# A hybrid decoder layer on one core: the side chains' loads and stores go through GpSimd's DMA queue instead of SyncE's

## The chip, the cores and the metric

The kernel runs on one core of one Trainium2 chip. The metric is the device time of one execution in microseconds (us), from runs of the whole program; smaller is better. A profile is one execution taken by the hardware profiler; its times are counted from the first instruction of the span.

## What is computed

One layer of a decoder, for 256 prompt tokens and 8 sample tokens (one new token of each of 8 sequences), all in float32:

```
h = rms_norm(x, norm_w);  z = h @ w_in                 # 4096 -> 14368 columns
A: sliding-window attention, 8 heads x 128             # qa, ka, va, ga
B: trailing means over 2/4/8/16 positions, 1024 wide   # u, gb
C: gated DeltaNet, 16 heads x 128                      # q, k, v (conv(4) + SiLU), g, a, b
   prompt: chunked form with a triangular solve
   sample: state = state * exp(g); delta = (v - k.state) * beta
           state = state + k (x) delta; o = q.state    # per head and sequence, 128 x 128
mix = concat[A * silu(ga), B * silu(gb), C_norm * silu(g)]
y = rms_norm(x + mix @ w_out, final_norm_w)            # 4096 -> 4096
```

Outputs are y, the prompt's keys, values, pooling and convolution inputs and its delta state, and for the sample tokens the caches with the new row put in: the attention caches (8 x 2048 x 1024 for keys and for values) are copied but for their oldest row, and the 16 x 8 delta states are read, updated and written.

## The kernel before

**The stream.** Everything is built around one stream of matmuls on TensorE. The 264 tokens are the moving operand. There are 113 output tiles of 128 columns for the input projection (in the order a/b, 16 of k, then q, v, g for each of 16 heads, then the attention's, then the pooling's) and 32 for the output projection, each with 32 contraction tiles, dealt out in chunks of 8. A float32 product is made of three matmuls (`emit_main`, L518): upper part of the weights by the upper part of x, upper by lower, lower by upper. The weights come as 1 MB loads of two chunks (`raw`, three slots; `emit_loads`, L456). ScalarE casts a chunk to its upper part `wh`, VectorE subtracts to get the lower part `wl` (`emit_split`, L488). `wh` and `wl` have HB = 4 buffers each, so the splits run up to three chunks ahead of the matmuls. A load into a slot is issued when the second chunk of the load before it in that slot has been split. Behind it comes, at a rate that depends on the phase, a piece of 0.5 MB of the caches' copy from HBM to HBM (`emit_copy`, L476).

**The side chains.** What the heads need beside the stream (convolutions, delta rule, attention, pooling) is written as Python generators, one for each head or part, that all work in one pool of SBUF, `arena`. Between the chunks of the stream `step` (L1395) lets each chain go on to its next `yield`, as far as a planner finds time for it. The planner (`Model`, L80) holds an estimated time for each engine and for the last write and use of every column. It lets a step in when VectorE and ScalarE would end it before the splits of the chunks ahead are due, less a margin of 2 us. All engines run their instructions in the order in which this planner issued them, and wait by semaphores.

**Sample half of the delta rule** (`sample`, L1046). Two workers take the 32 halves (16 heads, 4 sequences each) in turn. A half loads the state (`sdT`, 256 KB), k and q spread over all partitions from small arrays in HBM (`s_k`, `s_q`, 256 KB each), and for the first half of a head it first stores q to HBM (`s_q<-small`). It waits with `due` (L290) until the planner expects its last load. Then come four products with k on VectorE, scalings on ScalarE, four updates of the state, the store of the new state (`o_ds`, 256 KB), and four products with q. The same buffers then serve the worker's next half, so its `sdT` load waits for that store to land.

**Other side transfers.** `load_decay` loads a head's decay row, spread over the partitions (`s_gc`, 128 KB), twice for each head; `ev_conv` (L608) stores the convolution's inputs (`o_cv`) and loads the sample's (`scT`) after every eighth tile; `delta` stores the final state (`o_dp`); `attn_s` (L1184) loads cache rows (`kg`, `vg`) and stores the new ones; `pool_u` and `pool_g` load and store for the pooling.

**Queues before.** Except for a few constants at the start that are issued from GpSimd, and one from ScalarE, all DMAs are issued from SyncE, named `self.sy` and also `self.ld` (L201). It issues them in order. A DMA waits for its operands, and also for the DMA eight places before it on its queue, whose semaphore it takes over. GpSimd does small work otherwise: in `ev_conv` it clears and copies the convolution's border, which ScalarE's first ACTIVATE of the convolution reads, and keeps copies of the sample columns; it computes powers for the norms.

Of the kernel before, what the change touches and what calls it, by code (L numbers as in the profile page):

```python
# [12 lines left out]
NP = 256            # prompt tokens  # L13
NB = 8              # sample tokens (one per sequence)
NT = NP + NB
NK = 32             # contraction tiles of the model width
KC = 8              # contraction tiles per chunk
# [10 lines left out]
def tile_plan():  # L28
    """Order of the output tiles of the input projection: (kind, index)."""
    plan = [("ab", 0)] + [("k", h) for h in range(CH)]  # L30
    for h in range(CH):
        plan += [("q", h), ("v", h), ("g", h)]
    for h in range(AH):
        plan += [("qa", h), ("ka", h), ("va", h), ("ga", h)]
    for g in range(4):
        plan += [("u", 2 * g), ("u", 2 * g + 1), ("gb", 2 * g), ("gb", 2 * g + 1)]
    return plan
# [37 lines left out]
class Model:  # L75
    """Estimated times (us) of the engines' queues, and of every column's last write and last use."""
# [7 lines left out]
    def span(self, ap):  # L84
        """The quarters of the partitions and the columns of a tile (the kernel's inputs and outputs are not followed)."""
# [31 lines left out]
    def op(self, eng, dur, outs, ins):  # L117
        t = max(self.t[eng], self.ready(outs, ins))
        # engines take turns at a PSUM bank
# [12 lines left out]
    def dma(self, out, in_):  # L132
        n = 4
        for x in out.shape:
            n *= x
        t = max(self.t["sy"], self.ready([out], [in_])) + .46
        self.t["sy"] = t
        self.t["dma"] = max(self.t["dma"], t + .65) + max(n / 359e3, .02)
        t = self.t["dma"] + .9
        self.done(t, [out], [in_])  # L140
        return t


class Meter:
    """An engine, with an estimate of the time that its instructions take (us)."""
# [5 lines left out]
    def __getattr__(self, name):  # L151
        f = getattr(self.eng, name)

        def run(*a, **k):
            if name == "dma_start":
                if self.key == "sy":
                    self.b.loaded = self.b.model.dma(k["out"], k["in_"])
# [21 lines left out]
class Chain:  # L179
    """A generator, the estimated time at which its last step is through, and its products yet to be issued."""  # L180
# [10 lines left out]
class Builder:  # L191
    def __init__(self, nc, tc, d, pools):
# [8 lines left out]
        self.sy = self.ld = Meter(self, "sy", nc.sync, 0.0, 0.0, 0.0)  # L201
# [44 lines left out]
    def get_all(self, *sizes):  # L246
        """All of them or none, so that no two chains wait for each other's space."""
# [42 lines left out]
    def due(self, loaded):  # L290
        """Until a load can be expected to be there."""
# [7 lines left out]
    def lose(self, t):  # L299
        """Time for ScalarE's tables."""  # L300
# [4 lines left out]
    def mm(self, out, lhsT, rhs, start=True, stop=True):  # L305
        """A side product: it is issued inside a later chunk of the stream."""
# [14 lines left out]
    def flush(self, every=True):  # L321
        """The side products whose operands can be expected to be there."""
# [74 lines left out]
    def late_const(self):  # L397
# [4 lines left out]
        # halves: silu(z) = (tanh(z/2) + 1) * z/2  # L402
        self.ts(self.cw, self.cw, 0.5, ALU.mult)
        # buffers of the delta-rule phase
# [12 lines left out]
    def setup_stream(self):  # L417
        self.chunks = []      # (m, first k tile, number of k tiles, load index, offset in the load's tiles)
        self.loads = []       # (m, first k tile, number of k tiles, last chunk served, place, load that frees it)
# [36 lines left out]
    def emit_loads(self, limit=None):  # L456
        """The loads whose place is free."""
# [54 lines left out]
    def main_bank(self, m):  # L512
        """The PSUM bank of an output tile, and the tile that had it before."""
# [4 lines left out]
    def emit_main(self, n):  # L518
# [3 lines left out]
        for i in range(nk):  # L522
# [8 lines left out]
            if m == 0:  # L531
                # rows 0 to 63: W's upper part by x; rows 64 to 127: its lower part by x's upper part
# [22 lines left out]
    def square_x(self, q):  # L555
        """Squares of four of the k tiles, summed into self.ssum."""
# [51 lines left out]
    def ev_conv(self, kind, h, ps):  # L608
# [18 lines left out]
        if cj == 7:  # L627
            self.sy.dma_start(out=self.d["o_cv"][:, ci * 88:(ci + 1) * 88], in_=cstage)
# [31 lines left out]
    def ev_ab(self, ps):  # L660
# [13 lines left out]
        # a_log -> -exp(a_log)  # L674
# [23 lines left out]
        self.sy.dma_start(out=self.s_gc, in_=a[0:CH, 0:NP])  # L698
        self.sy.dma_start(out=self.s_eb[0], in_=a[0:CH, NP:NT])
        self.sy.dma_start(out=self.s_eb[1], in_=a[32:48, NP:NT])  # L700
# [21 lines left out]
    def decay(self, h, gcb, D):  # L722
        """D[j, t, i] = exp(gc_i - gc_j) for i >= j, else 0."""
# [58 lines left out]
    def invert(self):  # L782
        """T = (I + A)^-1 of the 128 diagonal 32 x 32 blocks, one block per partition."""
# [32 lines left out]
    def assemble(self, hb):  # L816
        """E = T^T of the 128 x 128 tiles, from its 32 x 32 diagonal blocks, in place of U."""
# [90 lines left out]
    def delta(self, h, R, kd, D, o, S, X, sq):  # L908
# [60 lines left out]
        self.sy.dma_start(out=self.d["o_dp"][h], in_=S.ap[:, w[1]])  # L969
# [4 lines left out]
        # 128 eps (sum q^2 + eps)  # L974
# [19 lines left out]
        # the last reader of k, U and E has been issued: their place takes the head's output  # L994
# [16 lines left out]
    def sample_tab(self):  # L1011
        """Columns by (head, sequence), then rows on all partitions: e^g, k2 e^g beta, k beta."""
# [33 lines left out]
    def sample(self, h, f, Sb, kb, qb, jk, sm):  # L1046
# [4 lines left out]
        if f == 0:  # L1051
            self.sy.dma_start(out=self.s_q[h].rearrange("f d b -> d f b"),
# [24 lines left out]
        self.sy.dma_start(out=self.d["o_ds"][h, :, f * 512:(f + 1) * 512], in_=Sb.ap)  # L1077
# [91 lines left out]
    def have(self, k, buf):  # L1169
        """Row tile k of the mixed heads; those of attention come in two parts."""  # L1170
# [13 lines left out]
    def attn_s(self, h, rep):  # L1184
# [27 lines left out]
        for name, i in (("o_wk", 1), ("o_wv", 2)):  # L1212
            self.sy.dma_start(out=self.d[name][:, 2047, h * P:(h + 1) * P],
# [78 lines left out]
    def pool_u(self, t):  # L1292
# [3 lines left out]
        self.sy.dma_start(out=self.d["o_u"][t], in_=u.ap)  # L1296
# [72 lines left out]
    def load_res(self, i):  # L1369
        self.ld.dma_start(out=self.xr[i % 2].ap.rearrange("p (k n) -> p k n", k=4),  # L1370
                          in_=self.d["xT"][:, 4 * i:4 * i + 4, :])

    def finish_early(self):
        """What the last norm needs of the tiles but one."""
# [20 lines left out]
    def step(self, free=False):  # L1395
        """Each side chain goes on by a step, as far as VectorE and ScalarE have time beside the stream."""
# [39 lines left out]
    def tile_done(self, m):  # L1436
# [24 lines left out]
        else:  # L1461
            self.start(self.ev_plain(kind, i, ps), True)
            if kind == "va":
                def out_kv(i=i):
                    yield from self.wait(("va", i))
                    self.sy.dma_start(out=self.d["o_ka"][i], in_=self.z["ka", i].ap)
                    self.sy.dma_start(out=self.d["o_va"][i], in_=self.z["va", i].ap)
# [16 lines left out]
    def build(self):  # L1484
# [8 lines left out]
        # TensorE's clock rises while it is busy  # L1493
# [113 lines left out]
# the first output tiles go side by side through the contraction, while x comes in  # L1607
# [4 lines left out]
# pieces of the caches' copy per load of weights: keys' tiles, delta rule, attention, pooling, output  # L1612
# [137 lines left out]
```

## Time and profile before

| | before |
|---|---|
| median of 3 runs | 1835.51 us (1834.74 to 1837.76) |
| profiled execution, span from first to last instruction | 1828.2 us |
| around that span, against the median | 7.3 us |
| busy: TensorE (PE) | 1801.3 us, 99% |
| busy: VectorE (DVE) | 1298.7 us, 71% |
| busy: ScalarE (ACT) | 850.3 us, 47% |
| busy: GpSimd (POOL) | 192.8 us, 11% |
| moved by DMA | 519.66 MB, mean 284 GB/s; SyncE's queue 80.5% of the 16 DMA engines' time |

A share of busy time is an average over stages with different limits. A matmul counts as busy for longer than the next one takes to start behind it, so TensorE's 99% says that it seldom stands still, not that it runs at its peak. Where it stands still is read from views of single stages, from the list of waits (who waited, for whom, for how long), and from the queue of the engine that issues DMAs (SPq for SyncE's). The time of an idle engine that nobody waits for costs nothing.

### The profile page before, as it was taken

What the parts mean: (1) busy time and instruction counts of PE and PEld (TensorE: products, weight loads), DVE (VectorE), ACT (ScalarE), POOL (GpSimd) and SP (SyncE); (2) the same over time, 40 slices, a digit from 0 to 9 for tenths busy, and PEclk for the clock granted to TensorE, in tenths of its full rate; (3) what the DMA queues carried; (4) which work ended last, traced back from release to release, by engine and by line L of the source; (5) the groups of instructions that cost most, each with busy time, mean ns of one, the idle gap of its engine ahead of it and who ended that gap; (6) DMA issues with size and microseconds to landing.
All of it is one profiled execution on the core that took longest, in us unless ns stands there. A gap on an engine that the chain in (4) does not pass through costs nothing.

```text
span 1828.2 us, 38217 instructions
## 1 busy us (share of the span) xinstructions
PE 1801.3 (99%) x15120; PEld 1790.3 (98%) x15120; DVE 1298.7 (71%) x3155; ACT 850.3 (47%) x1442; POOL 192.8 (11%) x504
## 2 busy tenths in 40 slices
PE   9999999999999999999999999999999999999996
PEld 9999999999999999999999999999999999999995
DVE  7987879668789788787877778676655654444444
ACT  7644444455455455455544443434333444444442
POOL 1132560421011101111000000000000000000000
PEclk9999999999999999999999999999999999999998
DMA  9788897656787888879888888889888798888873
GB/s 322 263 289 295 272 234 260 237 198 234 262 327 269 286 305 313 304 267 319 323 312 306 313 308 297 284 283 333 306 299 288 274 339 302 295 294 303 297 240 118
DMA packets 109380, 519.66 MB, mean 284 GB/s; under 512 B 25408, under 2 KB 35872, under 8 KB 70272
## 3 DMA queue, kind: packets, MB, share of 16 engines
q1 hardware_dynamic: 108624, 516.71, 80.5%
q8 instruction: 118, 1.93, 0.4%
q0 software_dynamic: 432, 0.50, 0.1%
q14 instruction: 62, 0.51, 0.1%
q10 hardware_dynamic: 144, 0.02, 0.0%
HBM read 499.67 MB, written 152.50 MB: 357 GB/s over the span
## 4 chain that ended last, share of the span: by engine, by line
PE 88%; DVE 5%; DMA 4%; issue 1%; ACT 1%; SPq 1%; DVEq 0%; ACTq 0%
PE mps L540 27%; PE mps L541 27%; PE mps L542 27%; PE sps L307 4%; DVE arena L174 3%; DMA raw<-win 3%; DVE wl L174 2%; PE sps L311 1%; PE sps L541 1%; PE sps L540 1%; PE sps L542 1%; SPq L158 1%; DVE y L174 1%; DMA o_ds<-arena 0%; ACT wh L174 0%
## 5 line engine op out<-in xcount | busy, mean ns | idle before, releaser
L540 PE MATMUL mps<-xh,wh 128*128 128x264 f32 x3456 | 995.3, 288 | 2.0 <-ACT wh L174 2.0
L542 PE MATMUL mps<-xh,wl 128*128 128x264 f32 x3456 | 979.9, 284 | 1.7 <-DVE wl L174 1.6
L174 DVE TENSOR_TENSOR wl<-raw,wh 128x1024 fp32r<-128x1024 f32 (+1 forms) x581 | 704.5, 1214 | 389.7 <-ACT wh L174 382.4
L541 PE MATMUL mps<-xl,wh 128*128 128x264 f32 x3456 | 980.2, 284 | 0.0
L174 ACT CAST wh<-raw 128x1024 fp32r<-128x1024 f32 (+2 forms) x586 | 604.8, 1036 | 611.2 <-PE mps L541 471.7
L540 PEld LDWEIGHTS mps<-xh,wh 128*128 128x128 f32 x3456 | 652.1, 189 | 3.7 <-ACT wh L174 2.5
L541 PEld LDWEIGHTS mps<-xl,wh 128*128 128x128 f32 x3456 | 651.7, 189 | 0.2
L542 PEld LDWEIGHTS mps<-xh,wl 128*128 128x128 f32 x3456 | 648.8, 188 | 2.5 <-DVE wl L174 2.5
L174 DVE SCALAR_TENSOR_TENSOR arena<-arena 128x128 f32<-128x128 f32 (+5 forms) x882 | 264.6, 356 | 10.9 <-DMA arena<-s_k 4.2
L174 ACT ACTIVATE arena<-arena 128x128 f32<-128x128 f32 (+7 forms) x319 | 119.3, 401 | 143.3 <-DVE arena L174 140.8
L542 PE MATMUL mps<-mix,wl 128*128 128x264 f32 x512 | 145.7, 284 | 0.0
L542 PE MATMUL mps<-mixc,wl 128*128 128x264 f32 x512 | 145.7, 284 | 0.0
L540 PE MATMUL mps<-mixc,wh 128*128 128x264 f32 x512 | 145.5, 284 | 0.0
L540 PE MATMUL mps<-mix,wh 128*128 128x264 f32 x512 | 145.5, 284 | 0.0
L541 PE MATMUL mps<-mixc,wh 128*128 128x264 f32 x512 | 144.9, 283 | 0.0
L541 PE MATMUL mps<-mix,wh 128*128 128x264 f32 x512 | 144.8, 283 | 0.0
L174 POOL COPY arena<-arena 128x8 f32<-128x8 f32 (+5 forms) x192 | 67.8, 376 | 450.7 <-DVE arena L174 392.8
L540 PEld LDWEIGHTS mps<-mix,wh 128*128 128x128 f32 x512 | 96.2, 188 | 0.0
L540 PEld LDWEIGHTS mps<-mixc,wh 128*128 128x128 f32 x512 | 96.2, 188 | 0.0
L542 PEld LDWEIGHTS mps<-mixc,wl 128*128 128x128 f32 x512 | 96.1, 188 | 0.0
L542 PEld LDWEIGHTS mps<-mix,wl 128*128 128x128 f32 x512 | 96.1, 188 | 0.0
L541 PEld LDWEIGHTS mps<-mixc,wh 128*128 128x128 f32 x512 | 96.1, 188 | 0.0
(115 smaller groups left out, 1340.9 us busy)
## 6 DMA issues: line engine op xcount, KB each, us to landing
raw<-win SPq DMA_DIRECT2D x214, 1024.0 KB, 7.0
o_wk<-ck SPq DMA_DIRECT2D x128, 511.8 KB, 7.4
o_wv<-cv SPq DMA_DIRECT2D x128, 511.8 KB, 6.8
raw<-wout SPq DMA_DIRECT2D x58, 1024.0 KB, 5.3
arena<-kg SPq DMA_DIRECT2D x32, 320.0 KB, 6.7
arena<-vg SPq DMA_DIRECT2D x32, 320.0 KB, 7.1
arena<-sdT SPq DMA_DIRECT2D x32, 256.0 KB, 4.5
arena<-s_k SPq DMA_DIRECT2D x32, 256.0 KB, 4.5
```

The source lines that it names most:

```text
L158: return f(*a, **k)
L174: return f(*a, **k)
L307: self.put(lambda: self.t.matmul(out, lhsT=lhsT, rhs=rhs, start=start, stop=stop), out, [lhsT, rhs], 2)
L311: self.put(lambda: self.t.transpose(out, in_, self.ident[:k, :k]), out, [in_], 1)
L540: self.t.matmul(ps, lhsT=h[:, w], rhs=xh, start=(k == 0), stop=False)
L541: self.t.matmul(ps, lhsT=h[:, w], rhs=xl, start=False, stop=False)
L542: self.t.matmul(ps, lhsT=l[:, w], rhs=xh, start=False, stop=(k == NK - 1))
```

## The change

All transfers that belong to side chains move from SyncE's queue to GpSimd's: `self.ld` now means GpSimd, and stores of side chains that were written as `self.sy` become `self.ld`. SyncE keeps x, the weights, the caches' copies, the residual (`load_res`), the store of all k (`s_k<-small`), two copies of small states and the final output. The planner gets a formula for DMAs of GpSimd's queue: they occupy GpSimd for 0.6 us and land 2.0 us plus twice their bytes at 359 GB/s later. Comments are taken out.

```diff
@@ Model
-    def dma(self, out, in_):
+    def dma(self, out, in_, queue="sy"):
         n = 4
         for x in out.shape:
             n *= x
+        if queue == "g":
+
+            t = self.t["g"] = max(self.t["g"], self.ready([out], [in_])) + .6
+            self.t["dma"] += n / 359e3
+            t += 2.0 + 2 * n / 359e3
+            self.done(t, [out], [in_])
+            return t
         t = max(self.t["sy"], self.ready([out], [in_])) + .46
@@ Meter
-                if self.key == "sy":
-                    self.b.loaded = self.b.model.dma(k["out"], k["in_"])
+                if self.key in ("sy", "g"):
+                    self.b.loaded = self.b.model.dma(k["out"], k["in_"], self.key)
@@ Builder
-        self.sy = self.ld = Meter(self, "sy", nc.sync, 0.0, 0.0, 0.0)
+
+        self.sy = Meter(self, "sy", nc.sync, 0.0, 0.0, 0.0)
+        self.ld = self.g
@@ sample
-            self.sy.dma_start(out=self.s_q[h].rearrange("f d b -> d f b"),
+            self.ld.dma_start(out=self.s_q[h].rearrange("f d b -> d f b"),
...
-        self.sy.dma_start(out=self.d["o_ds"][h, :, f * 512:(f + 1) * 512], in_=Sb.ap)
+        self.ld.dma_start(out=self.d["o_ds"][h, :, f * 512:(f + 1) * 512], in_=Sb.ap)
@@ load_res
-        self.ld.dma_start(out=self.xr[i % 2].ap.rearrange("p (k n) -> p k n", k=4),
+        self.sy.dma_start(out=self.xr[i % 2].ap.rearrange("p (k n) -> p k n", k=4),
```

The same edit from `self.sy` to `self.ld` stands at the stores `o_cv`, `s_gc`, `s_eb`, `o_dp`, `o_wk` and `o_wv` (the new row), `o_u`, `o_ka` and `o_va`. The loads `sdT`, `s_k`, `s_q`, `s_gc`, `scT`, `s_eb`, `kg`, `vg`, `abias`, `spT` and `pw` were written with `self.ld` before and go along.

How the queues change in the sample half of the delta rule. SyncE before, some 490 to 510 us into the span; `win` are the weights, `ck` the cache that is copied, and the names in brackets are the semaphores waited for (DMAHW: an earlier DMA of SyncE, DVE: VectorE):

```order
L158 DMA raw_80<-win 128x2048 [waits DMAHW0_49,DVE_49]
L158 DMA o_wk<-ck 16x8188 [waits DMAHW1_49]
L158 DMA o_ds<-arena 128x512 [waits DMAHW2_49]
L158 DMA arena<-sdT 128x512 [waits DMAHW3_49,DMAHW2_49,DVE_49]
L158 DMA arena<-s_k 128x512 [waits DMAHW4_49]
L158 DMA s_q<-small 128x2x4 [waits DMAHW5_49]
L158 DMA arena<-s_q 128x512 [waits DMAHW6_49,DMAHW5_49]
L158 DMA raw_81<-win 128x2048 [waits DMAHW7_49,DVE_49]
L158 DMA o_wk<-ck 16x8188 [waits DMAHW0_49]
L158 DMA o_ds<-arena 128x512 [waits DMAHW1_49,DVE_49]
L158 DMA raw_79<-win 128x2048 [waits DVE_49]
```

SyncE in the changed kernel, in the same part of the program:

```order
L165 DMA raw_80<-win 128x2048 [waits DMAHW7_49,DMAHW5_49,DVE_49]
L165 DMA o_wk<-ck 16x8188
L165 DMA raw_81<-win 128x2048 [waits DMAHW1_49,DVE_49]
L165 DMA o_wk<-ck 16x8188 [waits DMAHW0_49]
L165 DMA raw_79<-win 128x2048 [waits DMAHW3_49,DVE_49]
L165 DMA raw_80<-win 128x2048 [waits DMAHW5_49,DMAHW2_49,DVE_49]
```

Between two weight loads stood a store, three loads and a store of q; now there is at most a copy.

GpSimd before, in the same part; `MEMSET arena 128x3` and the `COPY` of 128x8x3 behind it make the convolution's border:

```order
L174 COPY small<-arena 128x8 [waits DVE_49]
L174 MEMSET arena 128x3
L174 COPY arena<-arena 128x8x3 [waits PE_49]
L174 COPY arena<-arena 128x3 [waits DVE_49]
L174 COPY arena<-arena 128x8 [waits DVE_49]
```

GpSimd in the changed kernel; DMASW is an earlier DMA of GpSimd:

```order
L181 COPY small<-arena 128x8 [waits DVE_49]
L165 DMA arena<-sdT 128x512 [waits DMASW6_49,DMASW1_49]
L165 DMA arena<-s_k 128x512 [waits DMASW2_49]
L165 DMA s_q<-small 128x2x4 [waits DMASW3_49]
L165 DMA arena<-s_q 128x512 [waits DMASW4_49,DMASW3_49]
L165 DMA o_ds<-arena 128x512 [waits DMASW5_49,DVE_49]
L181 MEMSET arena 128x3 [waits PE_49,Activation_49]
L181 COPY arena<-arena 128x8x3 [waits Pool_49]
L181 COPY arena<-arena 128x3 [waits DVE_49]
L181 COPY arena<-arena 128x8 [waits DVE_49]
```

The half's loads and stores, with their waits for each other, now stand ahead of the convolution's border copy.

## Rows read from the trace of the kernel before

**Rows 1.** Busy us by stage: PE, PEld, DVE, ACT, POOL (count), clock, DMA share, GB/s

```profile
25.00:475.00 450.00, 450.00 (x4056) 447.16 (x4055) 361.12 (x802) 226.80 (x380) 131.94 (x337) 1.00 0.77 260
475.00:1000.00 525.00, 517.78 (x4270) 514.71 (x4269) 430.64 (x1294) 270.00 (x567) 50.30 (x138) 1.00 0.84 299
1000.00:1800.00 800.00, 800.00 (x6563) 797.13 (x6563) 480.09 (x1017) 334.49 (x461) 5.45 (x16) 1.00 0.83 292
```

**Rows 2.** Timeline of TensorE, two matmuls after a hole: start, us, [idle before <-releaser]

```profile
606.39 0.39 PE L540 MATMUL mps<-xh,wh 128*128 128x264 f32 x1 [1.82 <-ACT wh L174]
...
607.65 0.59 PE L542 MATMUL mps<-xh,wl 128*128 128x264 f32 x1 [0.75 <-DVE wl L174]
```

**Rows 3.** Busy time as in rows 1, of that hole and behind it

```profile
604.00:608.00 4.00, 1.43 (x8) 1.00 (x7) 1.58 (x2) 2.71 (x5) 0.00 (x0) 0.94 0.86 250
608.00:612.00 4.00, 4.00 (x24) 4.00 (x24) 2.44 (x9) 1.37 (x4) 0.30 (x1) 0.63 1.03 432
```

**Rows 4.** Waits from 475 to 1000 us: us in total, times, longest

```profile
DVE wl L174 <- ACT wh L174: 74.8, 49, 6.9
ACT wh L174 <- DMA raw<-win: 70.6, 27, 8.1
...
DVE arena L174 <- DMA arena<-s_k: 4.2, 2, 3.3
DVE arena L174 <- DMA arena<-s_gc: 3.4, 1, 3.4
...
ACT arena L174 <- POOL arena L174: 2.6, 1, 2.6
```

**Rows 5.** Waits of SyncE's DMA queue, 475 to 1000 us

```profile
SPq L158 <- DMA o_ds<-arena: 134.2, 25, 10.5
SPq L158 <- DVE arena L174: 104.5, 63, 5.5
SPq L158 <- DMA s_q<-small: 53.2, 14, 6.0
SPq L158 <- DVE wl L174: 48.0, 25, 6.3
SPq L158 <- DMA raw<-win: 17.6, 8, 3.7
```

**Rows 6.** Timeline of SyncE's queue: start, us of the issue, what

```profile
494.51 0.43 SPq L158 DMA_DIRECT2D s_q<-small  x1
498.67 0.32 SPq L158 DMA_DIRECT2D arena<-s_q  x1
499.08 0.38 SPq L158 DMA_DIRECT2D raw<-win  x1
...
500.12 0.78 SPq L158 DMA_DIRECT2D o_ds<-arena  x1
...
509.19 0.34 SPq L158 DMA_DIRECT2D arena<-sdT  x1
...
510.58 0.38 SPq L158 DMA_DIRECT2D raw<-win  x1
```

**Rows 7.** Chain of work through 485 to 525 us, shares by line

```profile
by line: DMA o_ds<-arena 22.6%; DVE arena L174 21.7%; DMA arena<-s_q 14.6%; DMA s_q<-small 10.4%; DVE wl L174 8.7%; SPq L158 6.7%; issue 6.4%; ACT wh L174 2.6%; PE mps L540 2.1%; PE mps L542 1.8%; PE mps L541 1.8%; PE sps L311 1.3%; ACT are
```

**Rows 8.** Timeline of GpSimd, a DMA that it issues

```profile
74.74 0.54 POOL L158 DMA_DIRECT2D arena<-scT  x1 [3.41 <-PE sps L307]
```

**Rows 9.** DMAs issued from GpSimd, whole run: count, KB each, median us to landing

```profile
arena<-scT POOLq DMA_DIRECT2D x2, 96.0 KB, 6.7
...
arena<-cmask POOLq DMA_DIRECT2D x1, 64.0 KB, 10.4
```

**Rows 10.** DMAs issued from SyncE, 475 to 1000 us, columns as in rows 9

```profile
o_ds<-arena SPq DMA_DIRECT2D x28, 256.0 KB, 10.5
...
arena<-s_gc SPq DMA_DIRECT2D x10, 128.0 KB, 10.1
...
o_cv<-arena SPq DMA_DIRECT2D x3, 44.0 KB
```

More of the change, by code (lines that the diff above doesn't have):

```diff
@@ L627, in ev_conv @@
         if cj == 7:
-            self.sy.dma_start(out=self.d["o_cv"][:, ci * 88:(ci + 1) * 88], in_=cstage)
+            self.ld.dma_start(out=self.d["o_cv"][:, ci * 88:(ci + 1) * 88], in_=cstage)
             if ci + 2 < 6:
@@ L697, in ev_ab @@
         self.s_eb = self.drp.tile([2, CH, NB], F32, name="s_eb")
-        self.sy.dma_start(out=self.s_gc, in_=a[0:CH, 0:NP])
-        self.sy.dma_start(out=self.s_eb[0], in_=a[0:CH, NP:NT])
-        self.sy.dma_start(out=self.s_eb[1], in_=a[32:48, NP:NT])
+        self.ld.dma_start(out=self.s_gc, in_=a[0:CH, 0:NP])
+        self.ld.dma_start(out=self.s_eb[0], in_=a[0:CH, NP:NT])
+        self.ld.dma_start(out=self.s_eb[1], in_=a[32:48, NP:NT])
         self.rel(one, wk)
@@ L968, in delta @@
         self.stt(S.ap[:, w[1]], S.ap[:, w[0]], col(self.egl, 1), b[:, P:NP], ALU.mult, ALU.add)
-        self.sy.dma_start(out=self.d["o_dp"][h], in_=S.ap[:, w[1]])
+        self.ld.dma_start(out=self.d["o_dp"][h], in_=S.ap[:, w[1]])
         self.relb(b)
@@ L1212, in attn_s @@
         for name, i in (("o_wk", 1), ("o_wv", 2)):
-            self.sy.dma_start(out=self.d[name][:, 2047, h * P:(h + 1) * P],
+            self.ld.dma_start(out=self.d[name][:, 2047, h * P:(h + 1) * P],
                              in_=qkv.ap[0:P:16, i * P:(i + 1) * P])
@@ L1295, in pool_u @@
         u = self.z["u", t]
-        self.sy.dma_start(out=self.d["o_u"][t], in_=u.ap)
+        self.ld.dma_start(out=self.d["o_u"][t], in_=u.ap)
         sp, p, f, n0, n1 = yield from self.get_all(120, NT, 32, NP, NP)
@@ L1465, in out_kv @@
                     yield from self.wait(("va", i))
-                    self.sy.dma_start(out=self.d["o_ka"][i], in_=self.z["ka", i].ap)
-                    self.sy.dma_start(out=self.d["o_va"][i], in_=self.z["va", i].ap)
+                    self.ld.dma_start(out=self.d["o_ka"][i], in_=self.z["ka", i].ap)
+                    self.ld.dma_start(out=self.d["o_va"][i], in_=self.z["va", i].ap)
                     rep = yield from self.get(384)
```

## The prediction

> **What bounds the kernel now.** I read the busy time by stage first. Between 25 and 475 us and between 1000 and 1800 us TensorE is busy for all of the 450.00 and 800.00 us [rows 1]: its own matmuls set the time there, 800 us / 6563 = 0.122 us each, so 24 x 0.122 = 2.9 us for a chunk of eight contraction tiles, and nothing that a queue does can make those stretches shorter. The start, the last norm and the output's stores are not touched. What is left to win lies in the middle, from 475 to 1000 us, where the sample half of the delta rule runs: 525.00 - 517.78 = 7.2 us without a matmul [rows 1].
>
> Next comes the largest of these holes. TensorE stands 1.82 and 0.75 us, for a cast of weights on ScalarE and for VectorE's remainder [rows 2]; in the 4 us of the hole the granted clock is 0.94, and in the 4 us behind it 0.63, a mean of stretches at 1.2 and at 2.4 GHz after an engine that had been idle [rows 3]. That costs 4 x 0.37 + 4 x 0.06 = 1.7 us more. So the stage loses 7.2 + 1.7 = 8.9 us. This is all that the change can give back.
>
> Third, who is late? In this stage ScalarE's casts wait 70.6 us for `raw`, and VectorE's splits 74.8 us for ScalarE [rows 4]: most of VectorE's 525 - 430.64 = 94.4 us of idle time [rows 1] is there because weights come late. The weights are late because SyncE, which issues its DMAs in order, stands in front of something else: 134.2 us for an `o_ds` store to land, 104.5 us for VectorE's side work, 53.2 us for an `s_q` store, and only 48.0 us because a slot isn't free and 17.6 us for `raw` loads under way [rows 5]. One such stretch, row by row: an `s_q` store at 494.51, its reload only at 498.67, a weight load behind it at 499.08; an `o_ds` store at 500.12, the load into its buffer at 509.19, and the next weight load at 510.58 [rows 6]. The chain of work through that stretch is made of these: `o_ds` 22.6%, the `s_q` load 14.6%, the `s_q` store 10.4% [rows 7].
>
> **The change part by part.** *SyncE's queue.* It loses the loads and stores of the side chains and keeps weights and copies, whose only waits are for a slot and for transfers eight places earlier; the first two pieces of order show it. Of the waits in rows 5, 134.2 + 104.5 + 53.2 = 291.9 of 357.5 us are for side work and leave this queue, 82%. The holes don't tell their causes apart finely enough for more, so I take the same share of the loss: 0.82 x 8.9 = 7.3 us back. The ends: nothing (if the holes come from VectorE's load alone), and all 8.9 us.
>
> *GpSimd's queue.* It gets about 320 DMAs; one takes it 0.54 us [rows 8], some 170 us in 1828, and in this stage it is busy for 50.30 of 525 us [rows 1], so the issuing itself is hidden in idle time. If GpSimd were full, each would delay what stands behind it by 0.54 us. What is not hidden is the waiting, which moves along: `arena<-sdT` still waits for `o_ds`, `arena<-s_q` for `s_q<-small`, now in front of GpSimd's small copies. The last piece of order shows what is queued there: the memset and the copy of a convolution's border, for which ScalarE's next convolution waits, then the weights' casts behind that.
>
> *When side loads land.* The planner now counts 0.6 us of issue, 2.0 us and twice 256 KB / 359 GB/s = 1.5 us, 4.1 us in all. No row shows a 256 KB load on GpSimd's queue. The nearest are its own small loads, of 96 KB after a median of 6.7 us and of 64 KB after 10.4 us [rows 9], 2.6 and 6.3 us later than that. A half of the sample work holds back until its third load is due, one issue (0.6 us) after the second, which it needs first; so a half may find VectorE waiting for 2.0 to 5.7 us, and there are 28 halves (by their `o_ds` stores) in the stage [rows 10]: 56 to 160 us of VectorE. The price of VectorE standing still is read from the stage itself: 94.4 us of it went with 8.9 us of loss, 0.094 us for each. That makes 5.3 to 15 us. On the other side, late loads hardly showed so far: ten loads of `s_gc` landed after 10.1 us [rows 10], and VectorE waited 3.4 us for one of them and 4.2 us for `s_k` [rows 4], because a chain's next step usually comes a chunk later anyway. If the new loads land no later than these did, even those 7.6 us go, 0.7 us back. I take 2.0 us, near the lower end, because the ten `s_gc` loads are the row that shows what a late load does in this kernel; the range keeps both ends as far as the rivals do.
>
> The Trainium skill (SBUF — State Buffer, "SBUF: two separate sides") says that descriptors of a DMA issued from GpSimd cannot be written while VectorE holds the port that the two share, in its two-port modes. In rows 8 a GpSimd issue takes 0.54 us, with no operation of that kind beside it, so no run here shows the rule. If by that rule each half's load came later by as much as one issue takes, it would be an estimate of 28 x 0.54 x 0.094 = 1.4 us more than the sum below, 1831.6 us.
>
> *The other stages.* The `s_gc` loads of the first heads, the attention's `kg` and `vg` and the pooling's loads move too. I cost them at nothing: those stages have no hole now [rows 1], and VectorE has 450 - 361.12 and 800 - 480.09 us spare there. Without that cover a late load costs what it delays VectorE by, at most. The planner counts GpSimd's time now, so side steps are dealt out to other places in VectorE's order; the number of matmuls and of splits stays.
>
> *Sum.* -7.3 + 2.0 = -5.3 us. The profiled execution's span is 1828.2 us and the median of the runs 1835.51; the 7.3 us between lie outside the first and last instruction and stay. So **1830.2 us**, and from 1826 to 1832 for this case.
>
> **Rivals.** *The wait only moves.* GpSimd stands where SyncE stood, ScalarE and VectorE find it late now and then, and the loads' delay comes at its lower price of 5.3 us, not 2.0: -7.3 + 5.3, and half a hole of the size below, 2.1 us: 1835.6 us. For it: the same DMAs wait for the same landings. Against it: ScalarE waited for GpSimd for only 2.6 us in this stage [rows 4], and GpSimd's copies are few.
>
> *The weights stay late.* The queue isn't the limit but the DMA engines, which are busy for 0.84 of the stage [rows 1]; then weights wait for bytes, whoever asks for them, and the time stays at 1835.5 us. Against it: SyncE waits only 17.6 us for `raw` loads under way, and 291.9 us for side work [rows 5]. The Trainium skill (DMA: Bandwidth & Descriptors, "Rules for kernel authors") says that spreading DMAs over several issuing engines doesn't help bandwidth, since they share the DMA engines, and only saves issue time; by that rule this rival is the result, unless waiting in front of a DMA counts as issue time, which it leaves open.
>
> *GpSimd's queue stops ScalarE: slower.* A convolution's border copy stands behind `arena<-s_q`, which waits for a store and then for everything ahead of it on GpSimd's DMA queue. If that takes longer than the lead of TensorE's weights, three chunks or 8.7 us, ScalarE's in-order queue holds a cast back and TensorE has a hole like the one of rows 2 and 3, 1.82 + 0.75 + 1.7 = 4.3 us. There are 24 convolutions left in the stage (three `o_cv` stores of eight each, [rows 10]). Two such holes (8.6 us) undo the forecast's gain of 5.3 us; with three it is -5.3 + 12.9 = +7.6, **1843.1 us**. For it: 10.4 us for a GpSimd load in rows 9 and up to three stores and loads in a row on one queue. Against it: the step with the convolution comes a chunk after the one with the copy, and the planner counts GpSimd's waits.
>
> **Chances.** About 0.2%, 3.7 us, is what a measurement of this kernel can tell from no change. The forecast has 0.54, all of it faster by more than that. The moved wait has 0.16 and the late weights 0.08, both within 0.2%: 0.24. The stop on GpSimd has 0.22, slower. The range that should hold 8 in 10 goes from 1826 (all 8.9 us and the 0.7) to 1843 (three holes); what is left out is mostly more holes than that.
>
> **What will show it.** Right: SyncE's waits in this stage are for slots of `raw` and for older transfers only; ScalarE's 70.6 us for `raw` fall below 20; TensorE's idle time there falls from 7.2 to 3 us or less, and no stretch shows a clock of 0.63. The 2.0 us: VectorE waits for `sdT`, `s_k` or `s_gc` for some 20 us in all. The moved wait: ScalarE or VectorE waits for GpSimd for more than 20 us. The slower case: holes of TensorE behind a convolution's ACTIVATE that waits for GpSimd. Wrong altogether would be a loss in a stage that has no hole now, the first heads above all, where VectorE is at 0.80, or a median over 1843 us.

## The result and the profile after

The changed kernel takes **1923.66 us** (median of 4 runs, 1918.66 to 1926.79) against 1835.7 us for the kernel before on the same chip: ratio 1.0474, 95% interval 1.0453 to 1.0494. It is slower by some 88 us, where 5.3 us less was forecast and the range ended at 1843.

The span of the profiled execution is 1924.9 us, 96.7 us more than before. That is more than the 88 us of the medians because the changed kernel's profile is of the slowest of its four runs, and the kernel before's, with 1828.2 us, is shorter than the span of every timed run of that kernel on record (1831.1 us and more). In all these runs the time is 1.7 to 2.2 us more than the span, so most of the 7.3 us that the prediction laid outside the first and last instruction is not there; its forecast doesn't hang on it. The page's busy times, its shares by DMA queue and the chain that ended last:

```profile
PE 1834.0 (95%) x15120; PEld 1817.8 (94%) x15120; DVE 1302.8 (68%) x3155; ACT 849.2 (44%) x1442; POOL 368.7 (19%) x828
...
q1 hardware_dynamic: 62304, 451.12, 67.0%
q0 software_dynamic: 21200, 66.08, 11.2%
...
PE 62%; DMA 15%; DVE 10%; issue 8%; POOL 3%; ACT 2%; DVEq 0%; POOLq 0%; SPq 0%; ACTq 0%
```

The same 15120 matmuls keep TensorE busy for 1834.0 us, 32.7 us more than before, and it stands still for 64.0 us more (1924.9 - 1834.0 against 1828.2 - 1801.3). VectorE and ScalarE are busy for nearly the same time as before. So the loss is standing still, and the lower clock that TensorE has after it. By stage (columns: window, its length, busy us of PE, PEld, DVE, ACT and POOL with their counts, granted clock, DMA share, GB/s):

```profile
25.00:475.00 450.00, 447.26 (x4019) 444.05 (x4017) 359.08 (x784) 225.03 (x381) 156.08 (x383) 1.00 0.77 256
475.00:1000.00 525.00, 472.23 (x3716) 465.42 (x3715) 378.04 (x1131) 234.18 (x505) 131.15 (x289) 0.95 0.78 258
1000.00:1100.00 100.00, 88.52 (x679) 87.44 (x678) 78.13 (x304) 39.83 (x81) 23.92 (x47) 0.93 0.82 286
1100.00:1800.00 700.00, 695.98 (x5686) 692.52 (x5685) 411.37 (x843) 286.93 (x386) 52.45 (x97) 1.00 0.83 294
```

Beside [rows 1], the stage of the sample half has lost 52.8 us instead of 7.2 and its clock fell to 0.95; it has also grown past 1000 us. A few us are lost in stages that had no hole. The DMA engines' share fell, so bytes are not what is short.

What did the move do to the queue it was meant for? All that SyncE waits for between 475 and 1000 us (engine, line, what it waited for: us in total, times, longest):

```profile
SPq L165 <- DVE wl L181: 322.6, 47, 18.5
SPq L165 <- DVE arena L181: 138.9, 22, 14.5
```

Both rows stand in front of loads of `raw`, which wait for VectorE only until a slot has been split. The waits for `o_ds` and `s_q` of [rows 5] are gone, as is ScalarE's wait for `raw` of [rows 4], 70.6 us before and in no row now. The weights are early. Others wait instead, in the same stage:

```profile
POOL arena L165 <- DMA s_q<-small: 85.9, 12, 9.8
...
ACT arena L181 <- POOL arena L181: 52.9, 9, 13.7
DVE arena L181 <- DMA arena<-s_k: 47.8, 12, 9.0
...
POOL arena L165 <- DMA o_ds<-arena: 33.1, 8, 6.7
...
PE sps L316 <- DVE arena L181: 18.7, 8, 6.5
...
PE mps L551 <- DVE wl L181: 10.6, 5, 5.9
```

GpSimd stands for stores; ScalarE for GpSimd's border copies; VectorE for `s_k`, 47.8 us where it was 4.2; and TensorE for VectorE. One turn of this, first GpSimd's rows from 505 us on (start us, us, engine, line, operation, out<-in, and in brackets the idle time before it and who ended it):

```profile
505.00 0.59 POOL L165 DMA_DIRECT2D o_ds<-arena  x1
508.72 0.74 POOL L181 TENSOR_TENSOR arena<-arena,small 128x2 f32<-128x2 f32 x1 [3.13 <-DVE arena L181]
509.95 0.59 POOL L165 DMA_DIRECT2D arena<-sdT  x1 [0.48 <-DMA o_ds<-arena]
510.53 0.54 POOL L165 DMA_DIRECT2D arena<-s_k  x1
511.06 0.74 POOL L165 DMA_DIRECT2D s_q<-small  x1
518.29 0.56 POOL L165 DMA_DIRECT2D arena<-s_q  x1 [6.49 <-DMA s_q<-small]
518.85 0.55 POOL L165 DMA_DIRECT2D o_ds<-arena  x1
519.41 0.72 POOL L181 TENSOR_TENSOR arena<-arena,small 128x2 f32<-128x2 f32 x1
520.08 0.10 POOL L181 MEMSET arena<- 128x3 f32 x1
520.13 0.45 POOL L181 COPY arena<-arena 128x24 f32<-128x24 f32 x3
527.29 0.58 POOL L165 DMA_DIRECT2D arena<-sdT  x1 [6.71 <-DMA o_ds<-arena]
527.87 0.55 POOL L165 DMA_DIRECT2D arena<-s_k  x1
```

Then VectorE's row for that `s_k`, ScalarE's for the convolution behind the border copy, and TensorE's:

```profile
535.54 0.39 DVE L181 SCALAR_TENSOR_TENSOR arena<-arena 128x128 f32<-128x128 f32 x1 [8.27 <-DMA arena<-s_k]
```
```profile
520.36 0.54 ACT L181 ACTIVATE arena<-arena,small 128x288 f32<-128x288 f32 x1 [7.57 <-POOL arena L181]
```
```profile
537.81 0.59 PE L551 MATMUL mps<-xh,wl 128*128 128x264 f32 x1 [5.90 <-DVE wl L181]
```

The first worker's `s_q` store holds GpSimd for 6.49 us. Behind it stand the second worker's `o_ds`, issued only at 518.85, and hence, one landing later (6.71 us), its `sdT` and `s_k`; a border copy, too, stood in that queue (ScalarE 7.57 us). VectorE, in order, has come to the half's first step and stands 8.27 us; the next split of weights stands behind that, and TensorE for 5.90 us. The windows around this hole:

```profile
532.00:536.00 4.00, 0.00 (x0) 0.00 (x0) 0.46 (x3) 0.00 (x0) 0.00 (x0) 1.00 0.73 178
536.00:540.00 4.00, 2.19 (x10) 2.19 (x11) 3.97 (x16) 1.41 (x5) 1.40 (x4) 0.55 0.04 10
540.00:544.00 4.00, 4.00 (x23) 4.00 (x23) 3.93 (x8) 2.54 (x4) 0.00 (x0) 0.60 0.34 63
```

Behind the hole the clock is 0.55 and 0.60 of 2.4 GHz, a mean of stretches at 1.2 and 2.4. Over the whole trace TensorE has 29 holes over 0.3 us, 70.1 us together (counted from the rows of its matmuls between 25 and 1820 us): 19.6 us stand in front of the stream's own matmuls, and 50.5 us in front of side products (`sps`), which stand in TensorE's order between them.

### The profile page after: what moved, and what is told of

Same layout as the page of the kernel before. It is cut to its first block, busy times and chain, and to the rows that moved or that the text cites. A ratio compares the mean times of both kernels' runs of the same rounds, so it can differ in the third digit from the quotient of the medians.

```text
span 1924.9 us, 38265 instructions
## 1 busy us (share of the span) xinstructions
PE 1834.0 (95%) x15120; PEld 1817.8 (94%) x15120; DVE 1302.8 (68%) x3155; ACT 849.2 (44%) x1442; POOL 368.7 (19%) x828
## 4 chain that ended last, share of the span: by engine, by line
PE 62%; DMA 15%; DVE 10%; issue 8%; POOL 3%; ACT 2%; DVEq 0%; POOLq 0%; SPq 0%; ACTq 0%
PE mps L549 19%; PE mps L551 19%; PE mps L550 19%; DVE arena L181 6%; DMA arena<-s_k 3%; DVE wl L181 3%; DMA o_ds<-arena 3%; PE sps L316 3%; DMA arena<-vg 3%; DMA s_q<-small 3%; DMA arena<-kg 3%; POOL arena L165 2%; ACT wh L181 1%; POOL arena L181 1%; PE sps L550 1%
## 5 line engine op out<-in xcount | busy, mean ns | idle before, releaser
L549 PE MATMUL mps<-xh,wh 128*128 128x264 f32 x3456 | 1009.4, 292 | 8.3 <-ACT wh L181 8.3
L551 PE MATMUL mps<-xh,wl 128*128 128x264 f32 x3456 | 992.9, 287 | 11.4 <-DVE wl L181 11.3
L550 PE MATMUL mps<-xl,wh 128*128 128x264 f32 x3456 | 993.1, 287 | 0.0
L549 PEld LDWEIGHTS mps<-xh,wh 128*128 128x128 f32 x3456 | 665.3, 193 | 10.1 <-ACT wh L181 8.9
L551 PEld LDWEIGHTS mps<-xh,wl 128*128 128x128 f32 x3456 | 661.4, 191 | 13.2 <-DVE wl L181 13.2
L550 PEld LDWEIGHTS mps<-xl,wh 128*128 128x128 f32 x3456 | 664.5, 192 | 0.2
L181 DVE SCALAR_TENSOR_TENSOR arena<-arena 128x128 f32<-128x128 f32 (+5 forms) x882 | 265.2, 355 | 104.5 <-DMA arena<-s_k 52.5
L181 ACT ACTIVATE arena<-arena 128x128 f32<-128x128 f32 (+6 forms) x319 | 118.6, 402 | 225.7 <-DVE arena L181 224.9
L181 DVE SCALAR_TENSOR_TENSOR arena<-arena,small 128x288 f32<-128x288 f32 x144 | 74.6, 518 | 44.5 <-ACT arena L181 41.1
```

Of the source, the lines that this page charges most:

```text
L181: return f(*a, **k)
L549: self.t.matmul(ps, lhsT=h[:, w], rhs=xh, start=(k == 0), stop=False)
L550: self.t.matmul(ps, lhsT=h[:, w], rhs=xl, start=False, stop=False)
L551: self.t.matmul(ps, lhsT=l[:, w], rhs=xh, start=False, stop=(k == NK - 1))
```

## The experiments

All times are medians; the ratio is to the kernel before on the same chip.

| run | us | ratio (95% interval) |
|---|---|---|
| e1_order_only | 1916.01 | 1.0422 (1.0401 to 1.0443) |
| e2_queue_only | 1888.32 | 1.0261 (1.0232 to 1.0289) |
| e3_no_store_waits | 1908.84 | 1.0386 (1.0362 to 1.0409) |
| e4_planner_later | 1876.60 | 1.0214 (1.0194 to 1.0233) |
| e5_before_no_waits | 1829.66 | 0.9957 (0.9944 to 0.9970) |
| e8_queue_no_waits | 1842.39 | 1.0031 (1.0020 to 1.0042) |
| e9_later_no_waits | 1854.13 | 1.0090 (1.0075 to 1.0105) |
| e10_border_on_dve | 1866.39 | 1.0147 (1.0123 to 1.0171) |
| e11_stores_on_pool | 1825.87 | 0.9946 (0.9933 to 0.9959) |
| e12_later_on_sp | 1903.95 | 1.0371 (1.0357 to 1.0386) |
| e13_products_later | 1949.42 | 1.0627 (1.0607 to 1.0647) |
| e14_sp_products_later | 1833.31 | 0.9985 (0.9974 to 0.9995) |
| e15_before_early | 1892.19 | 1.0288 (1.0262 to 1.0314) |
| e16_after_due_later | 1894.15 | 1.0295 (1.0251 to 1.0339) |
| e17_due_later_no_waits | 1839.89 | 1.0015 (1.0000 to 1.0030) |

**The two halves of the change, apart.** The change does two things: it issues the DMAs elsewhere, and it gives the planner another estimate of them, which moves steps in the order of all engines.

```diff
# e1_order_only
-        self.ld = self.g
+        self.ld = Meter(self, "g", nc.sync, 0.0, 0.0, 0.0)
# e2_queue_only
-                if self.key in ("sy", "g"):
+                if self.key == "sy":
...
-        self.ld = self.g
+        self.ld = Meter(self, "sy", nc.gpsimd, 0.0, 0.0, 0.0)
```

> The changed kernel's order of instructions on TensorE, VectorE and ScalarE to the last row, with the side chains' DMAs issued by SyncE again at the same places of the program. Theory Q (GpSimd's queue stands for landings in front of the next loads): the loss goes, 1825 to 1850 us, within 15 us of the kernel before. Rival O (the new order, made because the planner now counts GpSimd's time, is what costs): the loss stays, 1905 to 1930 us.

> The kernel before's order on TensorE, VectorE and ScalarE to the last row, with the side chains' DMAs issued by GpSimd. Theory Q: the loss is there without the new order, and no smaller, since this order allows for no wait of GpSimd at all: 1900 to 1960 us. Rival O: 1830 to 1845 us, the time before.

Neither theory holds alone: 1916.0 us without GpSimd's queue, as rival O had it, and 1888.3 us without the new order, outside both ranges. In e1, the new order on SyncE's queue, VectorE waits for side loads for 85.4 us between 475 and 1100 us, against 8.4 in the kernel before:

```profile
DVE arena L181 <- DMA arena<-s_k: 55.8, 18, 7.9
...
DVE arena L181 <- DMA arena<-kg: 17.0, 4, 6.6
...
DVE arena L181 <- DMA arena<-vg: 7.3, 3, 4.4
...
DVE arena L181 <- DMA arena<-s_gc: 5.3, 4, 2.6
```

In e2 ScalarE waits for GpSimd and VectorE for `s_k` too (between 475 and 1000 us):

```profile
ACT arena L181 <- POOL arena L181: 43.3, 10, 13.0
...
DVE arena L181 <- DMA arena<-s_k: 18.2, 5, 10.4
```

**The waits for stores, and the planner's figure.** e3 takes the stores out of the loads' way without touching the queues or the planner's figures; e4 touches one of these figures alone. The order is planned anew in both.

```diff
# e3_no_store_waits
@@ sample
-        if f == 0:
-            self.ld.dma_start(out=self.s_q[h].rearrange("f d b -> d f b"),
...
@@ store_q, started by the convolution of a head's q, two steps behind it
+        self.s_q[h] = self.drp.tile([2, P, NB // 2], F32, name=f"s_q{h}")
+        self.ld.dma_start(out=self.s_q[h].rearrange("f d b -> d f b"),
...
             yield from self.sample(i // 2, i % 2, *bufs)
+            bufs[0], bufs[3] = bufs[3], bufs[0]
# e4_planner_later
-            t += 2.0 + 2 * n / 359e3
+            t += 5.0 + 2 * n / 359e3
```

> The changed kernel, but no load of the sample half stands behind a store's landing: each head's s_q goes to memory soon after its convolution, in a tensor of its own, and a half's state goes into the buffer that was scratch in the half before, while the old state's buffer becomes the scratch. The loads still take GpSimd's 5 to 7 us. Theory Q (it is the waits for the stores that chain the delays up): at least 60 of the 88 us come back, 1830 to 1863 us. Rival L (the loads' own landing, 5.3 to 6.4 us where the planner counts 4.1, is what stalls VectorE): less than 30 us come back, 1894 to 1925 us.

> The changed kernel with one figure of the planner altered: a DMA on GpSimd's queue is counted to land 3 us later (5.0 for 2.0 in the formula). Queue and waits are as in the changed kernel, the steps behind a load are put later in the order. Theory Q: GpSimd still stands for the same landings, so that a half takes as long, but VectorE and TensorE are given other work meanwhile: 1850 to 1895 us. Rival L (the planner is merely wrong by 2 to 3 us on each load): 1825 to 1845 us. If the order doesn't matter to it at all: 1910 us or more.

e3 gave back 15 of 88 us, which speaks for rival L; e4 gave back 47, inside what theory Q expected. The planner's figure does more than the waits, but not all. From here on the theory was P, two losses at once.

**Both cures together.** e8 is e2 with the edit of e3, e9 is e4 with it, and e5 is the kernel before with it (on SyncE).

> As e2_queue_only (side DMAs on GpSimd, planned with the landing times of the kernel before), and as in e3 no load stands behind a store's landing: s_q goes out early in a tensor per head, state and scratch change places. Theory P (two losses: the changed planner's landing times are too short and put VectorE's steps too early; and GpSimd stands for stores in front of loads and of the convolutions' border copies): with the old landing times and without the waits for stores both are gone, 1830 to 1848 us. Rival S (GpSimd's queue is slow or disturbed by VectorE whatever it waits for): 1870 to 1892 us, as e2.

> As e4_planner_later (GpSimd's DMAs counted 3 us later), and no load stands behind a store's landing, as in e3. Theory P: 1830 to 1850 us. Rival S: 1865 to 1882 us, as e4. If the waits for stores are what helps and not the planner's time, e3 should have shown it already (it gained 15 us).

> The kernel before, everything on SyncE's queue, but with s_q out early in a tensor per head and state and scratch changing places, so that SyncE no longer stands for stores in front of loads. If the holes of the kernel before come from SyncE's waits, as the prediction had it, some 7 of the 8.9 us come back: 1826 to 1832 us. If they come from VectorE's own load: 1834 to 1839 us.

With the planner's figures of the kernel before, taking away the waits for stores gives back 46 of the 52 us that GpSimd's queue costs (1888.3 to 1842.4; the order is planned anew with them); rival S falls. e9 missed its range by 4 us, but lies 70 us under the changed kernel. And e5 is faster than the kernel before. What SyncE waits for in e5 between 475 and 1000 us, and ScalarE's wait for `raw` there:

```profile
SPq L158 <- DVE arena L174: 178.7, 78, 10.1
SPq L158 <- DVE wl L174: 131.6, 42, 7.2
...
SPq L158 <- DMA o_ds<-arena: 1.1, 2, 0.9
SPq L158 <- DMA s_q<-small: 1.0, 1, 1.0
```
```profile
ACT wh L174 <- DMA raw<-win: 0.4, 1, 0.4
```

The 134.2 and 53.2 us of [rows 5] and ScalarE's 70.6 us [rows 4] are gone, and with them 7.6 us (1837.25 to 1829.66). e8 has e5's order on TensorE, VectorE and ScalarE to the last row and differs only in the queue: 12.7 us is what is left as the price of GpSimd's queue when it stands for no store's landing; what it consists of isn't shown.

**Is it ScalarE, stopped behind GpSimd?**

```diff
# e10_border_on_dve, beside e2
+        self.gv = Meter(self, "g", nc.vector, .1, .0023, .06)
...
-        self.g.memset(ext[:, 0:3], 0.0)
+        self.gv.memset(ext[:, 0:3], 0.0)
...
-        self.g.tensor_copy(out=st[:, :, 0:3],
+        self.gv.tensor_copy(out=st[:, :, 0:3],
```

> As e2_queue_only, but the small operations of a convolution that GpSimd did (memset and copies of the border, the staged columns, the copy of the sample columns) are done by VectorE at the same place in the program, so that ScalarE's convolution waits for no GpSimd instruction that stands behind a DMA. The pow of the prompt half stays on GpSimd. If the stop of ScalarE behind GpSimd's queue is most of e2's 52 us: 1840 to 1863 us. If late loads and the pow are: 1875 to 1895 us.

It fell between its two ranges: 22 of e2's 52 us come back. That is the share of the border copies and the other small copies, less what 240 more instructions cost VectorE. What is left acts in other ways. One is shown: e10 keeps the longest hole that TensorE has in e2, 10.5 us where e2 has 11.0, both up to 468.6 us, and in it GpSimd stands 8.91 us for an `o_ds` store ahead of its `pow` of the prompt half, for which VectorE waits 10.24 us. How the rest divides between late loads and `pow` isn't shown.

**How the lateness reaches TensorE.** Since most of the lost time stood in front of side products, e13 puts each 5 us later in TensorE's order, and e14 1 us later in e5's; e12 is e4's order on SyncE's queue.

```diff
# e13_products_later (e14: -1.0, beside e5)
-PE_SLACK = 0.0
+PE_SLACK = -5.0
```

> The order of e4_planner_later (landings counted 3 us later) on TensorE, VectorE and ScalarE to the last row, with the side DMAs issued by SyncE at the same places: beside e1_order_only (1916 us) only the 3 us differ. Theory P (it is the short landing time that spoils the order): 1836 to 1858 us. If what spoils it is that the planner counts GpSimd's time, or no longer counts SyncE's: 1890 us or more.

> The changed kernel, queues and landing times as they are, but a side product is put into TensorE's stream only 5 us after the planner takes its operands to be there. In the changed kernel 20 of 29 holes of TensorE over 0.3 us, 50.5 of 70.1 us, stand in front of a side product. If that is how a late load reaches TensorE (its side products stand in order in the stream of the weights): 30 us or more come back, 1850 to 1894 us. If the lateness reaches it through the weights' casts and splits anyway: 1905 us or more.

> As e5_before_no_waits (1829.7 us), but a side product is put into TensorE's stream 1 us after the planner takes its operands to be there. All its holes over 0.3 us, 8 with 6.1 us, stand in front of side products: if they go, 1823 to 1828 us; if the steps behind the products come late in turn, 1829 to 1836 us.

All three came out as the second reading in each expectation had it. In e13 the holes in front of side products did not shrink (56.4 us after 50.5), and those in front of the stream's own matmuls grew from 19.6 to 35.5: later products don't help while VectorE itself stands, since the splits of weights stand behind it as well. Why it is 26 us worse than the changed kernel I didn't settle. e14 is 3.7 us slower than e5. In e12 VectorE's waits for side loads fell to 18.9 us between 475 and 1100 us, from 85.4 in e1, but only 12 us came back. SyncE's standing doesn't explain the rest: it stands 107.9 us for `o_ds` between 440 and 1200 us and 58.1 for `s_q`, and ScalarE 87.5 us for `raw`, where the kernel before has 136.9, 58.3 and 79.1. The longest hole of TensorE in e12, 19.4 us in front of a side product, ends with VectorE's steps of the attention, whose `kg` loads come late (13.6 us of the chain of work from 985 to 1025 us). How e12's 68 us divide stays open, and with it what the planner's figure is worth without GpSimd's queue; that the planner counts GpSimd's time, the expectation's other cause, was not tried by itself.

**VectorE's place in the order.** What was left to separate is the place of VectorE's first steps behind a load. `SOON` sets it, for `s_gc`, the sample half and also, beyond what the expectations name, the attention's `kg` and `vg`; the planner then deals the other steps out around them.

```diff
# e15_before_early: the kernel before
-SOON = 0.5
+SOON = 5.0
# e16_after_due_later: the changed kernel; e17: e3 with the same
-SOON = 0.5
+SOON = -4.0
```

> The kernel before, all on SyncE, with one figure altered: the steps behind a load of s_gc or of the sample half are let go 4.5 us sooner (5.0 us ahead of the time at which the planner counts on the load, not 0.5). Nothing of GpSimd's queue is in it. Theory P (VectorE, put too early, stands for loads in order, and with it the splits and TensorE's own side products): 1860 to 1930 us. If a late load is cheap, as the prediction priced it (0.094 us for each us that VectorE stands): 1836 to 1848 us.

> The changed kernel, with the steps behind a load of s_gc or of the sample half held back until 4.0 us after the planner counts on the load (0.5 us ahead of it in the changed kernel). Stores, GpSimd's time and all queues as in the changed kernel. Theory P: VectorE's waits for s_k and s_gc mostly go, and 30 to 70 us come back, 1854 to 1894 us; what stays are GpSimd's waits for stores. If those steps' places in the order don't matter: 1910 us or more.

> As e3_no_store_waits (1908.8 us: no load behind a store's landing), with the steps behind a load held back as in e16. Theory P: both losses are met, 1834 to 1860 us, near e9 (1854) and e8 (1842). If e9's gain came from another use of its 3 us (the stores' buffers, attention's loads): 1880 us or more.

All three came as theory P had it, e16 at the edge of its range. e15 costs 55 us with all side transfers on SyncE's queue, as in the kernel before; VectorE's waits in it and, second, in e17 (475 to 1000 us):

```profile
DVE arena L174 <- DMA arena<-s_k: 75.2, 18, 10.9
...
ACT wh L174 <- DMA raw<-win: 25.8, 8, 8.9
...
DVE arena L174 <- DMA arena<-s_gc: 8.2, 2, 6.0
```
```profile
DVE arena L181 <- DMA arena<-s_k: 10.3, 6, 3.6
...
ACT arena L181 <- POOL arena L181: 7.4, 3, 3.9
```

Beside the changed kernel, taking away the waits for stores gives 15 us back, holding VectorE's steps back 30 us, and both 84 of the 88 us: each alone leaves the other to stop TensorE. The planner of e17 still counts GpSimd's time, and e17 is within 3 us of the kernel before, so on GpSimd's queue that counting isn't what costs. In e16 VectorE's wait for `s_k` fell to 11.3 us, but ScalarE still waits 50.6 us for GpSimd.

**A version that beats both.** e11 is e5 with only those stores issued by GpSimd that nobody in the kernel reads.

```diff
# e11_stores_on_pool, beside e5
+        self.st = Meter(self, "sy", nc.gpsimd, 0.0, 0.0, 0.0)
...
-        self.sy.dma_start(out=self.d["o_ds"][h, :, f * 512:(f + 1) * 512], in_=Sb.ap)
+        self.st.dma_start(out=self.d["o_ds"][h, :, f * 512:(f + 1) * 512], in_=Sb.ap)
```

The stores of `o_dp`, `o_cv`, `o_ka`, `o_va`, `o_u` and of the new rows of `o_wk` and `o_wv` likewise.

> As e5_before_no_waits (1829.7 us), in the same order on TensorE, VectorE and ScalarE, but the stores of results that nobody in the kernel waits for (o_ds, o_dp, o_cv, o_ka, o_va, o_u and the new rows of o_wk and o_wv) are issued by GpSimd; all loads stay on SyncE. If what SyncE still loses is its standing for VectorE in front of those stores, with weights behind: 1826 to 1830 us. If a store that waits for VectorE in front of a border copy costs more on GpSimd: 1832 to 1843 us.

1825.87 us: 10 us (0.5%) under the kernel before and 98 under the changed one. Most of it is e5's: e11's ratio and e5's overlap in their intervals, so it isn't shown that moving those stores adds to it. The cure for SyncE's standing was to remove what it stood for; moving what nobody waits for did no harm.

## Why the prediction was wrong

**SyncE's queue, -7.3 us: right in its mechanism, its size near by some luck.** The waits left the queue, the weights came early, and ScalarE's 70.6 us for `raw` fell to nothing. e5, which takes the waits for stores away on SyncE itself, is 7.6 us faster than the kernel before. But e5 is planned anew, its matmuls in another order from the 3804th on, and the two profiles don't show where the 7.6 us went: TensorE stands for 26.9 us in the kernel before and 27.0 in e5 (7.2 and 4.8 in the stage of the sample half). The share was read wrong, too: of the 104.5 us that [rows 5] put down to VectorE's `arena` work, 72.9 stand in front of loads of `raw`. They are waits for a slot, which don't leave the queue, so that 219.0 of 357.5 us do, and the same sum gives 5.5 us.

**When side loads land, +2.0 us (ends -0.7 and 15): the step that failed.** The loads landed a little sooner than in the nearest rows: 5.6 us (`sdT`), 6.2 (`s_k`), 6.0 (`s_q`), 6.4 (`s_gc`), medians. What failed is what was made of it, in three ways.

- *The price.* 0.094 us for each us that VectorE stands was an average over its idle time in the kernel before, which lay for the most part in short waits for ScalarE's casts (74.8 us in 49 pieces [rows 4]). A wait for `s_k` is longer (up to 9.0 us) and holds the splits and the operands of side products together. e15 gives a price, if all of its loss is put down to such waits: VectorE's waits for side loads between 475 and 1100 us rose from 8.4 to 98.0 us, and the time by 55.3 us, 0.62 for each. By the same reckoning e1 gives 1.03 (to 85.4 us, and 79.2 us of time). The 2.0 us at 0.094 stood for 21 us of waits; the stage had 49 us for `s_k` and `s_gc`.
- *The cover.* I took the lower end because late `s_gc` loads hardly showed before, a chain's next step coming a chunk later anyway. (The 10.1 us of [rows 10] is the median of four of the ten loads, 8.1 to 10.8 us; the trace doesn't tell the landing of the others.) But it comes later because the planner puts it there, and the change altered the planner's estimate together with the queue. By the planner's own figures `s_k` lands 4.1 us after the end of `sdT`'s issue; it landed after 6.2 (median of 32) and up to 10.3. In the kernel before these are 4.9 planned, 4.6 and 5.8 measured, on the five loads whose landing the trace tells. I wrote the 4.1 us down as a delay of a few us for each load, and not as an order in which VectorE arrives early every time.
- *The landings in a row.* The two workers go in step: a store's landing, a load behind it, then the other worker's. I priced each load by its own landing, not by the queue in front of it.

**GpSimd's queue, no term in the sum: wrong too.** I hid the issuing in idle time and saw that the waiting moves along, but gave it nothing outside the rivals. By e2 and e8 the waits for stores are worth some 46 us.

**The other stages at nothing: wrong in size.** 2.7 us between 25 and 475 us, 11.5 between 1000 and 1100, 4.0 behind. The first of these are the early steps too, and not GpSimd's queue: VectorE stands 6.97 us for an `s_gc` load at 119 us, and TensorE 1.97 and 0.75 us behind it; e1 has this hole without GpSimd's queue, and e2, without the new order, and e4 have not. The sample half's loads begin before 475 us, at 413 us in e2, which loses 12.2 us between there and 475, and in the changed kernel they run past 1000 us, so these stages don't part its loss cleanly.

**The rivals.** "The wait only moves" was right in its mechanism and far too small in its price. "GpSimd's queue stops ScalarE" was seen word for word: 52.9 us of ScalarE behind border copies, in pieces of up to 13.7 us. It was priced as three holes, 12.9 us; e10 measures it, in the order of the kernel before, at 22 net of VectorE's added work. It was never the only loss: the two causes hide each other. "The weights stay late" fell: ScalarE no longer waits for `raw`, and the DMA engines' share went down to 0.78. The rule there, that spreading DMAs over issuing engines doesn't help bandwidth (the Trainium skill, DMA: Bandwidth & Descriptors, "Rules for kernel authors"), agrees with e11: with the stores on another engine the stage moved 304 GB/s, with all on SyncE 302 (e5).

**VectorE's lock on GpSimd's descriptors** (the Trainium skill, SBUF — State Buffer, "SBUF: two separate sides") left no trace in the issues: 32 each of `sdT` and `s_k` took 547 and 542 ns in the mean, as in [rows 8]. What e8 leaves, 12.7 us, is the most that it could cost there; no run separates it.

**Of the signs I named**, SyncE's waits and ScalarE's `raw` came as forecast; VectorE's waits for `s_k` and `s_gc` came to 49 us in that stage, not 20; TensorE's idle time rose instead of falling; and the loss in stages without a hole was the one that I had called wrong altogether.

## What to carry to other kernels

When a wait moves from a queue that computes nothing to one that also computes, ask what stands behind it there, for every engine in order; it is safer to remove the wait (store earlier, trade buffers) and to move only DMAs that nobody waits for. Where a planner sets the order, its estimate of a transfer is part of the change: one that is some us too short puts an in-order engine in front of a load each time, and the price of that was 0.62 and 1.03 us for each us of waiting in two runs here, not the 0.094 of its average idle time. And when one cure gives back little, try it together with the next before dropping it.

## What was not expected of the hardware

GpSimd's queue was not the slower one. In e11 the loads are on SyncE's queue, which no longer stands for stores, and they take longer to land than on GpSimd's queue in the changed kernel; in e8, which has e11's order on TensorE, VectorE and ScalarE and all side transfers on GpSimd's queue, they take about as long as in e11 (out<-in, queue, count, KB each, median us to landing; e11, the changed kernel, e8):

```profile
arena<-sdT SPq DMA_DIRECT2D x32, 256.0 KB, 7.4
arena<-s_k SPq DMA_DIRECT2D x32, 256.0 KB, 7.9
...
s_q<-small SPq DMA_DIRECT2D x16, 4.0 KB, 7.1
```
```profile
arena<-sdT POOLq DMA_DIRECT2D x32, 256.0 KB, 5.6
arena<-s_k POOLq DMA_DIRECT2D x32, 256.0 KB, 6.2
...
s_q<-small POOLq DMA_DIRECT2D x16, 4.0 KB, 6.4
```
```profile
arena<-sdT POOLq DMA_DIRECT2D x32, 256.0 KB, 6.5
arena<-s_k POOLq DMA_DIRECT2D x32, 256.0 KB, 7.6
...
s_q<-small POOLq DMA_DIRECT2D x16, 4.0 KB, 7.3
```

The e11 medians are of 23, 25 and 11 DMAs whose landing the trace tells, the others of all. What sets the landing isn't shown: the DMA engines were busier in e11 and e8, 0.87 and 0.85 of the stage against 0.78 in the changed kernel, and the order differs too. The kernel before seems to have had shorter ones on SyncE's queue, which kept standing for stores (4.5 us for `sdT`, 3.0 for the store of `s_q`), but its trace tells the landing of only one of the 32 `sdT` loads and one of the 16 stores, so that a queue which has just stood still lands its loads sooner isn't shown. And e11, with longer landings than the changed kernel, is the fastest kernel here: its order, by the planner's figures, counts on `s_k` 6.7 us after the end of `sdT`'s issue, where the changed kernel counts on 4.1.
